# A recurrence's decay from tanh and exp instead of a reciprocal, and sigmoids as tanh of half the argument

## The chip, the cores and the metric

The kernel runs on one NeuronCore of a Trainium2 chip. Each core has a matrix engine (TensorE, PE in the profile; PEld is its weight load), a vector engine (VectorE, DVE), an engine for functions by table (ScalarE, ACT), GpSimd (POOL), and SyncE (SP), whose queue issues most of the transfers here. Each engine works through its own list of instructions in order, and waits on semaphores for the others. The metric is the device time of one execution in microseconds (us), as the median of several runs.

## The reference

One layer of a streaming encoder on 512 frames of 1024 channels, all in float32: a gated token mixer, then a retrieval over 16384 small experts, each added to the residual, and a last RMS norm. The change lies in the second half of the mixer's heads, a gated linear recurrence over the frames:

```python
def rg_lru(xr, w_r, b_r, w_i, b_i, lam):
    b, s, _ = xr.shape
    xh = xr.reshape(b, s, N_LRU_HEADS, LRU_HD)
    r = jax.nn.sigmoid(jnp.einsum('bshi,hij->bshj', xh, w_r) + b_r).astype(jnp.float32)
    i = jax.nn.sigmoid(jnp.einsum('bshi,hij->bshj', xh, w_i) + b_i).astype(jnp.float32)
    log_a = -LRU_C * r * jax.nn.softplus(-lam.astype(jnp.float32))
    a = jnp.exp(log_a)
    u = jnp.sqrt(-jnp.expm1(2.0 * log_a)) * (i * xh.astype(jnp.float32))
...
    _, h = lax.associative_scan(combine, (a, u), axis=1)
    return h.reshape(b, s, LRU_W).astype(xr.dtype)
```

So h(t) = a(t) h(t-1) + u(t), with the decay a between 0 and 1 and u scaled by the root of 1 - a squared. The retrieval that follows scores 128 keys on two sides for each of 8 heads, takes the best 16 pairs, and sums the chosen experts.

## The kernel before

The program has four parts on the time line: a prologue (the frames' norm, the first part of the conditioning vector), the mixer, the scores and searches with the first expert products, and the products with the second expert table.

The mixer keeps channels on the 128 partitions and the 512 frames in the free dimension. Its input projection has 20 blocks of 128 output channels. A block is 24 matmuls of 128x512: weights and input are split into a high and a low part, and the loop over 8 slices of input channels makes three products each (`mm3`, lines 89 to 91: high by high, high by low, low by high). The loop of line 359 goes over four channel blocks `cb` of 128; each takes five of the 20 weight blocks, `px` (the recurrence's input), `pgr` (its output gate), `pc`, `pxa` and `pb` (the short convolution's three). They land in PSUM tiles `ps_z`, of which there are three. A weight block is loaded by SP (line 70, `wraw`), its high part copied by ACT (line 75, `whi`), its low part made by DVE (line 80, `wlo`); there are four buffers of each.

Inside one `cb` the recurrence runs so: ACT copies `px` (364, 366), DVE adds the four taps of the convolution (368, three operations), ACT and DVE split the sum `xc` (373, 375), TensorE makes the two gate products in `ps_g` (377 to 379), ACT makes the two sigmoids `r` and `ig` (381, 383) and `s` = tanh(sp r) (385), where `sp` is half of 8 softplus(-lambda). From s the decay is a = 2/(1+s) - 1, and the root of 1 - a squared is 2 sqrt(s)/(1+s): DVE takes the reciprocal `q` of 1+s (387, 388), `a` from it (390), and the products for u (392 to 394); ACT takes the square root (391). DVE scans over the frames (396), multiplies with the gelu of `pgr` (397 to 407, tanh form), and `head_norm` (333) squares the result on ACT, averages it over each head by two matmuls (341, 342) and scales it. The results of all heads, split into `ybuf_h` and `ybuf_l`, are the input of the output projection (428 to 435).

Beside this stands the rest of the conditioning vector. Its last third (`ada_group(2)`) is summed on DVE: a block `wacc` loaded (line 135) and scaled (151), then seven blocks `wada` added to it (153, three buffers), then a product with ones on TensorE (139), a copy on ACT (159) and transposes (162); and that twice.

The order of the mixer's instructions on each engine isn't written out: a scheduler of the framework places the instructions by its own estimate of their cost, and each engine then keeps that list. From line 1083 on the order is written by hand. ACT's functions come from tables; where the next one is not in the table set that is loaded, the list holds an ACT_TABLE_LOAD.

Of the kernel before, what the change touches and what calls it, by code (L numbers as in the profile page):

```python
# [8 lines left out]
F32 = mybir.dt.float32  # L9
# [4 lines left out]
AF = mybir.ActivationFunctionType  # L14
OP = mybir.AluOpType
# [19 lines left out]
def block_kernel(ctx, tc, xT, small, w_ada1, w_ada, b_ada, w_in, w_r, w_i, w_out, w_q, keys, uT, u, v, final_g, out):  # L35
    nc = tc.nc
    PS = bass.MemoryType.PSUM

    const = ctx.enter_context(tc.tile_pool(name="const", bufs=1))
# [4 lines left out]
    def sm(name, lo=0, n=None):  # L44
        o, w = SMALL[name]
        return small_sb[:, o + lo:o + lo + (w if n is None else n)]
# [9 lines left out]
    boot.close()  # L56
    iota = const.tile([128, 128], F32, name="iota")
    nc.gpsimd.iota(iota, pattern=[[1, 128]], base=0, channel_multiplier=0, allow_small_or_imprecise_dtypes=True)
    const.tile([128, 24], F32, name="pad")
    ones = const.tile([128, 1], F32, name="ones")  # L60
    nc.vector.memset(ones, 1.0)
    sel2 = const.tile([128, XB], F32, name="sel2")
# [195 lines left out]
    sp = const.tile([128, 4], F32, name="sp")  # L258
# [21 lines left out]
    nc.vector.tensor_scalar(z_, lam, -1.0, 0.0, op0=OP.mult, op1=OP.max)  # L280
    nc.vector.tensor_scalar(ac, ac, 8.0, None, op0=OP.mult)
    nc.vector.scalar_tensor_tensor(sp, z_, 4.0, ac, op0=OP.mult, op1=OP.add)
    g2d = dram.tile([2, 512], F32, name="g2d")
    mx = ExitStack()
    mixp = mx.enter_context(tc.tile_pool(name="mixp", bufs=1))
# [33 lines left out]
    def zblock(n, name):  # L319
        i = order.index(n)  # L320
        for j in range(i, min(i + ZL + 2, len(order))):
            if order[j] not in raws:
                raws[order[j]] = load_w(w_in[order[j]])
        for j in range(i, min(i + ZL, len(order))):
            if order[j] not in zsp:
                zsp[order[j]] = split_w(raws[order[j]])
        hi, lo = zsp[n]
        ps = psZ.tile([128, T], F32, name=name, bufs=3)
        mm3(ps, hi, lo, hx, lx, range(KB), True, True)
        next(ada_it, None)  # L330
        return ps
# [27 lines left out]
    for cb in range(4):  # L359
        px = zblock(12 + cb, "ps_z")  # L360
        if pend:
            head_norm(*pend.pop())
        mt = lambda n: mix.tile([128, T], F32, name=n)
        nc.scalar.activation(xpad[:, 3:], px, AF.Copy)
        xc = mt("xc")
        nc.scalar.activation(xc, px, AF.Identity, scale=sm("cbw", cb * 4 + 3, 1), bias=sm("cbb", cb, 1))
        for k in range(3):
            nc.vector.scalar_tensor_tensor(xc, xpad[:, k:k + T], sm("cbw", cb * 4 + k, 1), xc, op0=OP.mult, op1=OP.add)
        pgr = zblock(16 + cb, "ps_z")
        pg = psZ.tile([128, T], F32, name="ps_g", bufs=2)  # L370
        pi = psZ.tile([128, T], F32, name="ps_g", bufs=2)
        xch = mix.tile([128, T], FR, name="cg")
        nc.scalar.activation(xch, xc, AF.Copy)
        xcl = mix.tile([128, T], FR, name="acc")
        nc.vector.tensor_sub(xcl, xc, xch.bitcast(F32))
        for ps, b in ((pg, cb), (pi, 4 + cb)):
            nc.tensor.matmul(ps, bdh[:, b, :], xch, start=True, stop=False)
            nc.tensor.matmul(ps, bdh[:, b, :], xcl, start=False, stop=False)
            nc.tensor.matmul(ps, bdl[:, b, :], xch, start=False, stop=True)
        r = mt("r")  # L380
        nc.scalar.activation(r, pg, AF.Sigmoid, bias=sm("br", cb, 1))
        ig = mt("ig")
        nc.scalar.activation(ig, pi, AF.Sigmoid, bias=sm("bi", cb, 1))
        s = mt("s")
        nc.scalar.activation(s, r, AF.Tanh, scale=sp[:, cb:cb + 1])
        q = mt("q")
        nc.vector.tensor_scalar(q, s, 1.0, None, op0=OP.add)
        nc.vector.reciprocal(q, q)
        a = mt("r")
        nc.vector.tensor_scalar(a, q, 2.0, -1.0, op0=OP.mult, op1=OP.add)  # L390
        nc.scalar.activation(s, s, AF.Sqrt)
        nc.vector.tensor_mul(xc, xc, ig)
        nc.vector.tensor_mul(xc, xc, s)
        nc.vector.scalar_tensor_tensor(xc, xc, 2.0, q, op0=OP.mult, op1=OP.mult)
        h = mt("ig")
        nc.vector.tensor_tensor_scan(h, a, xc, 0.0, op0=OP.mult, op1=OP.add)
        x2 = mt("x2")
        nc.scalar.activation(x2, pgr, AF.Square)
        gr = mt("gr")
        nc.scalar.activation(gr, pgr, AF.Copy)  # L400
        nc.vector.tensor_scalar(x2, x2, 0.044715, 1.0, op0=OP.mult, op1=OP.add)
        nc.vector.tensor_mul(x2, x2, gr)
        nc.scalar.activation(x2, x2, AF.Tanh, scale=0.7978845608028654)
        nc.vector.scalar_tensor_tensor(x2, x2, 1.0, gr, op0=OP.add, op1=OP.mult)
        y = mix.tile([128, T], F32, name="y", bufs=2)
        pend.append((y, 4 + cb, sm("gnb", cb, 1)))
        nc.vector.scalar_tensor_tensor(y, x2, 0.5, h, op0=OP.mult, op1=OP.mult)
        pc = zblock(4 + cb, "ps_z")
        cg = mix.tile([128, T], F32, name="cg")
        nc.scalar.activation(cg, pc, AF.Copy)  # L410
        pxa = zblock(8 + cb, "ps_z")
        head_norm(*pend.pop())
        nc.vector.tensor_mul(vpad[:, 2:], pxa, cg)
        acc = mix.tile([128, T], F32, name="acc")
        nc.scalar.activation(acc, vpad[:, 2:], AF.Copy, scale=sm("caw", cb * 3 + 2, 1))
        for k in range(2):
            nc.vector.scalar_tensor_tensor(acc, vpad[:, k:k + T], sm("caw", cb * 3 + k, 1), acc, op0=OP.mult, op1=OP.add)
        pb = zblock(cb, "ps_z")
        y = mix.tile([128, T], F32, name="y", bufs=2)
        nc.vector.tensor_mul(y, acc, pb)  # L420
        pend.append((y, cb, sm("gna", cb, 1)))
# [64 lines left out]
    for k in range(KB):  # L486
# [4 lines left out]
                             bias=adac[:, 24 + k:25 + k])  # L491
# [678 lines left out]
    for k in range(CE, len(jobs)):  # L1170
# [6 lines left out]
        else:  # L1177
            q, e = divmod(n, 2)
# [137 lines left out]
```

## Time and profile before

| | us |
|---|---|
| median of 3 runs | 1362.52 (1361.08 to 1362.64) |
| the profiled execution's own time | 1361.49 |
| its span, first to last instruction | 1359.7 |
| busy in the span: PE, DVE, ACT, POOL | 1309.5, 1224.1, 729.4, 510.7 |
| DMA, mean over the span | 324 GB/s |

Times in the trace's rows are us from the span's start. A row of the timeline has start, length, engine, line, operation, output and inputs, shape, count, and in brackets how long the engine sat idle before it, and for whom. Instructions of one engine overlap a little, so that two rows may start closer together than the first is long. The mixer's blocks lie between about 44 and 218 us.

### The profile page before, as it was taken

To read this page: it belongs to the slowest core of one execution; us is meant where nothing else is said; L and a number is where in the kernel's file an instruction comes from. 1 tells how busy PE (TensorE), PEld (TensorE's weight loads), DVE (VectorE), ACT (ScalarE), POOL (GpSimd) and SP (SyncE) were. 2 spreads that over 40 slices of the span, in tenths; PEclk is the share of its full clock that TensorE was granted. 3 is DMA by queue.
4 is the path that set the end of the run, shared out by engine and by line. 5 is a ranking of instruction groups with operands and counts; after the bars stand their busy time and mean duration, and the time that the engine had idled before them with its cause. 6 is when DMAs were issued, how large, how long until landed. Compare 5 with 4: busy or idle time off the path is not lost.

```text
span 1359.7 us, 21251 instructions
## 1 busy us (share of the span) xinstructions
PE 1309.5 (96%) x7432; PEld 1120.9 (82%) x7432; DVE 1224.1 (90%) x2261; ACT 729.4 (54%) x1314; POOL 510.7 (38%) x336
## 2 busy tenths in 40 slices
PE   5999999999999999999999989999999999999996
PEld 2667687777999999999899988788888888888884
DVE  6889975889999999999889659799889889999998
ACT  4666644523576988798669544333333434333433
POOL 0000000000244133436557416577647665554550
PEclk9999998999999999999999999999999999999998
DMA  9676442251789999999999999999999999999993
GB/s 357 233 273 214 126 123 101 69 187 34 244 301 330 334 326 405 395 370 375 417 402 417 416 344 390 392 377 416 413 415 413 415 413 415 411 413 410 393 344 136
DMA packets 149375, 440.57 MB, mean 324 GB/s; under 512 B 14994, under 2 KB 42642, under 8 KB 149268
## 3 DMA queue, kind: packets, MB, share of 16 engines
q1 hardware_dynamic: 102116, 267.75, 52.8%
q0 software_dynamic: 46864, 170.41, 32.2%
q8 instruction: 58, 0.95, 0.3%
q10 hardware_dynamic: 288, 1.05, 0.2%
q14 instruction: 49, 0.40, 0.1%
HBM read 394.07 MB, written 45.09 MB: 323 GB/s over the span
## 4 chain that ended last, share of the span: by engine, by line
PE 59%; DVE 19%; DMA 9%; issue 9%; POOL 2%; ACT 1%; SPq 0%; DVEq 0%; POOLq 0%; ACTq 0%
PE acc L1153 33%; PE ps_z L89 4%; PE ps_z L90 4%; PE ps_z L91 4%; DVE wlo L80 4%; DMA wraw<-in_uT_dram 3%; PE ps_act L89 3%; PE ps_act L91 3%; PE ps_act L90 3%; DMA rows<-in_u_dram,idx_s 3%; DVE scr L880 2%; POOL rows L859 2%; DVE oh L692 2%; DMA wraw<-in_v_dram 1%; PE ps_gt L725 1%
## 5 line engine op out<-in xcount | busy, mean ns | idle before, releaser
L75 ACT ACTIVATE whi<-wraw 128x1024 fp32r<-128x1024 f32 x255 | 269.9, 1059 | 339.2 <-PE acc L1153 154.1
L80 DVE TENSOR_TENSOR wlo<-wraw,whi 128x1024 fp32r<-128x1024 f32 x255 | 310.7, 1219 | 61.2 <-ACT whi L75 60.5
L89 PE MATMUL ps_act<-h,whi 128*128 128x320 f32 x928 | 292.5, 315 | 0.0
L90 PE MATMUL ps_act<-h,whi 128*128 128x320 f32 x928 | 287.6, 310 | 0.0
L91 PE MATMUL ps_act<-h,wlo 128*128 128x320 f32 x928 | 287.6, 310 | 0.0
L859 POOL DMA_INDIRECT rows<-in_u_dram,idx_s x128 | 204.2, 1596 | 159.3 <-DVE scr L880 141.8
L859 POOL DMA_INDIRECT rows<-in_v_dram,idx_s x128 | 204.1, 1595 | 154.6 <-DVE ys L897 130.0
L1153 PE MATMUL acc<-whi,ch 128*128 128x512 f32 x750 | 232.9, 392 | 6.3 <-ACT ch L1039 5.2
L1153 PE MATMUL acc<-whi,cl 128*128 128x512 f32 x750 | 232.5, 391 | 0.0
L1153 PE MATMUL acc<-wlo,ch 128*128 128x512 f32 x750 | 232.1, 391 | 0.0
L89 PEld LDWEIGHTS ps_act<-h,whi 128*128 128x128 f32 x928 | 175.0, 189 | 0.7
L90 PEld LDWEIGHTS ps_act<-h,whi 128*128 128x128 f32 x928 | 174.9, 189 | 0.2
L91 PEld LDWEIGHTS ps_act<-h,wlo 128*128 128x128 f32 x928 | 174.7, 188 | 0.0
L859 POOL DMA_INDIRECT rows<-in_u_dram,idx_b x64 | 96.1, 1502 | 208.9 <-DVE scr L880 143.0
L1153 PEld LDWEIGHTS acc<-whi,ch 128*128 128x128 f32 x750 | 141.5, 189 | 36.3 <-ACT ch L1039 5.9
L1153 PEld LDWEIGHTS acc<-wlo,ch 128*128 128x128 f32 x750 | 141.6, 189 | 29.6
L1153 PEld LDWEIGHTS acc<-whi,cl 128*128 128x128 f32 x750 | 141.4, 189 | 29.7 <-DVE cl L1046 0.3
L897 DVE SCALAR_TENSOR_TENSOR ys<-rows,acts,ys 128x1024 f32<-128x1024 f32 x127 | 162.7, 1281 | 1.4
L880 DVE SCALAR_TENSOR_TENSOR scr<-rows,h2n 128x1024 f16<-128x1024 f32 x128 | 156.4, 1222 | 5.2 <-DMA rows<-in_u_dram,idx_s 3.6
L713 ACT ACTIVATE igh<-oh,gl 128x128 f16<-128x128 f16 x320 | 99.6, 431 | 14.5 <-DVE oh L692 14.4
L453 POOL DMA_DIRECT2D x1d<-xn x8 | 4.5, 569 | 257.8 <-ACT xn L452 257.8
L964 ACT ACTIVATE act<-ps_act 128x320 f32<-128x320 f32 x127 | 55.3, 435 | 77.7 <-PE ps_act L91 44.5
(305 smaller groups left out, 1912.3 us busy)
## 6 DMA issues: line engine op xcount, KB each, us to landing
wraw<-in_uT_dram SPq DMA_DIRECT2D x120, 512.0 KB, 7.4
wraw<-in_v_dram SPq DMA_DIRECT2D x103, 512.0 KB, 13.1
wada<-in_w_ada_dram SPq DMA_DIRECT2D x46, 512.0 KB, 5.4
Gd<-stg SPq DMA_DIRECT2D x46, 512.0 KB, 9.0
Ad<-act SPq DMA_DIRECT2D x48, 320.0 KB, 9.2
act<-Ad SPq DMA_DIRECT2D x48, 320.0 KB, 14.2
raw<-in_v_dram SPq DMA_DIRECT2D x25, 512.0 KB, 13.5
h<-Gd SPq DMA_DIRECT2D x12, 1024.0 KB, 17.8
```

The source lines that it names most:

```text
L75: nc.scalar.activation(hi, raw, AF.Copy)
L80: nc.vector.tensor_sub(lo, raw, hi.bitcast(F32))
L89: nc.tensor.matmul(ps, hi[:, k, :], xh(k), start=first and k == ks[0], stop=False)
L90: nc.tensor.matmul(ps, hi[:, k, :], xl(k), start=False, stop=False)
L91: nc.tensor.matmul(ps, lo[:, k, :], xh(k), start=False, stop=last and k == ks[-1])
L692: nc.vector.tensor_tensor(flat.rearrange("p (q n b) -> p q n b", q=8, b=2), io2[:, None, :, :].to_broadcast(shp), sij[:, a0].rearrange("p ...
L713: nc.scalar.activation(ig[:, 1, k // 2, :, k % 2], of[:, k // 2, 0, :, k % 2], AF.Copy, scale=gl[:, t0 + k:t0 + k + 1])
L859: nc.gpsimd.indirect_dma_start(out=r[:, :], out_offset=None, in_=table, in_offset=bass.IndirectOffsetOnAxis(ap=idxs[:, k:k + 1], axis=0))
L880: nc.vector.scalar_tensor_tensor(scr, rows.pop(n), 1.0, hn, op0=OP.mult, op1=OP.mult, accum_out=dst[:, k:k + 1])
L897: nc.vector.scalar_tensor_tensor(ys, rows.pop(k), acts[:, k:k + 1], ys, op0=OP.mult, op1=OP.add)
L964: nc.scalar.activation(act[c // 2][:, c % 2], ps, AF.Gelu)
L1153: nc.tensor.matmul(accs[b][e], st[:, bs], mv[:, e * 512:(e + 1) * 512], start=first, stop=last)
```

## The change

The decay is written with two functions instead of a reciprocal. With x = 8 softplus(-lambda) r, s = tanh(x/2) and q = exp(-x), (1+q) s = 1 - q, so that a = 1 - (1+q) s is q again, but carries s's accuracy near 1; and 1/(1+s) = (1+a)/2. Both sigmoids become tanh of half the argument: r and ig now hold 2 sigmoid - 1, and the missing "+1" and "/2" are moved into scales and biases (columns `sph`, `spn`, `brh`, `bih`, made once on 128x4) and into the operations that follow. The root is taken of s/4. The pad tile shrinks by the 16 columns that the new columns take, so that other tiles keep their places.

```diff
-    const.tile([128, 24], F32, name="pad")
+    const.tile([128, 8], F32, name="pad")
...
+    rg = const.tile([128, 4, 4], F32, name="rg")
+    sph, spn, brh, bih = (rg[:, i, :] for i in range(4))
+    for dst, src, f in ((sph, sp, 0.5), (spn, sp, -1.0), (brh, sm("br"), 0.5), (bih, sm("bi"), 0.5)):
+        nc.vector.tensor_scalar(dst, src, f, None, op0=OP.mult)
...
         r = mt("r")
-        nc.scalar.activation(r, pg, AF.Sigmoid, bias=sm("br", cb, 1))
+        nc.scalar.activation(r, pg, AF.Tanh, scale=0.5, bias=brh[:, cb:cb + 1])
         ig = mt("ig")
-        nc.scalar.activation(ig, pi, AF.Sigmoid, bias=sm("bi", cb, 1))
+        nc.scalar.activation(ig, pi, AF.Tanh, scale=0.5, bias=bih[:, cb:cb + 1])
         s = mt("s")
-        nc.scalar.activation(s, r, AF.Tanh, scale=sp[:, cb:cb + 1])
+        nc.scalar.activation(s, r, AF.Tanh, scale=sph[:, cb:cb + 1], bias=sph[:, cb:cb + 1])
         q = mt("q")
-        nc.vector.tensor_scalar(q, s, 1.0, None, op0=OP.add)
-        nc.vector.reciprocal(q, q)
+        nc.scalar.activation(q, r, AF.Exp, scale=spn[:, cb:cb + 1], bias=spn[:, cb:cb + 1])
         a = mt("r")
-        nc.vector.tensor_scalar(a, q, 2.0, -1.0, op0=OP.mult, op1=OP.add)
-        nc.scalar.activation(s, s, AF.Sqrt)
-        nc.vector.tensor_mul(xc, xc, ig)
+        nc.vector.scalar_tensor_tensor(a, q, 1.0, s, op0=OP.add, op1=OP.mult)
+        nc.vector.tensor_scalar(a, a, -1.0, 1.0, op0=OP.mult, op1=OP.add)
+        nc.scalar.activation(s, s, AF.Sqrt, scale=0.25)
+        nc.vector.scalar_tensor_tensor(xc, ig, 1.0, xc, op0=OP.add, op1=OP.mult)
         nc.vector.tensor_mul(xc, xc, s)
-        nc.vector.scalar_tensor_tensor(xc, xc, 2.0, q, op0=OP.mult, op1=OP.mult)
+        nc.vector.scalar_tensor_tensor(xc, a, 1.0, xc, op0=OP.add, op1=OP.mult)
```

From the first new lines on, a line n of the kernel before is line n + 4 of the changed one; in the recurrence's own lines the new ones are 385, 387, 389 (r, ig, s), 391 (Exp), 393, 394 (decay), 395 (root), 396 to 398 (u) and 400 (scan). The scheduler places the mixer anew, with the new costs; from the output projection's second half on, all lists are the same as before. Three places of the lists follow.

TensorE in the last block, `cb` 3, around its gate products (`ps_g`) and the second `wacc` product. Before, where `ps_z_1379`, `ps_z_1423` and `ps_z_1476` are the weight blocks 17, 18 and 19:

```order
L91 MATMUL ps_z_1303<-h2_83,wlo_1301 128x512
L89 MATMUL ps_z_1379<-h2_83,whi_1375 128x512
L90 MATMUL ps_z_1379<-h2_83,whi_1375 128x512
L89 MATMUL ps_z_1423<-h2_83,whi_1419 128x512
L90 MATMUL ps_z_1423<-h2_83,whi_1419 128x512
L89 MATMUL ps_z_1476<-h2_83,whi_1472 128x512
L90 MATMUL ps_z_1476<-h2_83,whi_1472 128x512
L377 MATMUL ps_g_1334<-cg_1336,bdh_380 128x512
L377 MATMUL ps_g_1335<-cg_1336,bdh_380 128x512
L139 MATMUL ps_row_946<-wacc_1166,ones_79 1x512 x2
L162 MATMUL ps_row_1408<-ident_73,row_1406 128x128 x4
```

In the changed kernel, where `ps_z_1384` and `ps_z_1428` are the weight blocks 17 and 18:

```order
L91 MATMUL ps_z_1384<-h2_83,wlo_1382 128x512
L381 MATMUL ps_g_1339<-cg_1341,bdh_385 128x512
L381 MATMUL ps_g_1340<-cg_1341,bdh_385 128x512
L89 MATMUL ps_z_1384<-h2_83,whi_1380 128x512
L90 MATMUL ps_z_1384<-h2_83,whi_1380 128x512
L91 MATMUL ps_z_1384<-h2_83,wlo_1382 128x512
L139 MATMUL ps_row_951<-wacc_1171,ones_79 1x512 x2
L89 MATMUL ps_z_1428<-h2_83,whi_1424 128x512
L382 MATMUL ps_g_1339<-acc_1343,bdh_385 128x512
```

The first pairs of three weight blocks stood ahead of the gate products; now nearly all of block 17 stands there (its `wlo` is made earlier on DVE), so that between the first `wacc` product and the gate products there are 97 matmuls of 128x512 where there were 82.

DVE at the same place, around the last of the seven additions to `wacc` (153) and the three convolution taps on `xc` (368; 372 in the changed kernel). Before:

```order
L352 TENSOR_TENSOR ybuf_l<-mfull,ybuf_h 128x512
L368 SCALAR_TENSOR_TENSOR xc<-xpad,small_sb,xc 128x512
L153 SCALAR_TENSOR_TENSOR wacc<-wada,cs,wacc 128x1024
L347 SCALAR_TENSOR_TENSOR sq<-ps_rs,sq 128x512
L368 SCALAR_TENSOR_TENSOR xc<-xpad,small_sb,xc 128x512
L348 SCALAR_TENSOR_TENSOR sq<-sq,mfull 128x512
L368 SCALAR_TENSOR_TENSOR xc<-xpad,small_sb,xc 128x512
L350 SCALAR_TENSOR_TENSOR mfull<-y,small_sb,sq 128x512
L153 SCALAR_TENSOR_TENSOR wacc<-wada,cs,wacc 128x1024
```

In the changed kernel:

```order
L343 SCALAR_TENSOR_TENSOR mt_1281<-sq,mt_1279 128x512
L372 SCALAR_TENSOR_TENSOR xc<-xpad,small_sb,xc 128x512
L153 SCALAR_TENSOR_TENSOR wacc<-wada,cs,wacc 128x1024
L372 SCALAR_TENSOR_TENSOR xc<-xpad,small_sb,xc 128x512
L153 SCALAR_TENSOR_TENSOR wacc<-wada,cs,wacc 128x1024
L351 SCALAR_TENSOR_TENSOR sq<-ps_rs,sq 128x512
L372 SCALAR_TENSOR_TENSOR xc<-xpad,small_sb,xc 128x512
L352 SCALAR_TENSOR_TENSOR sq<-sq,mfull 128x512
```

The last addition has moved ahead of the last tap.

ACT in the recurrence of `cb` 3. Before, from the second sigmoid on (`cg` is the copy of the next block's `pc`):

```order
L383 ACTIVATE ig<-ps_g,small_sb 128x512
L385 ACTIVATE s<-r,sp 128x512
L403 ACTIVATE x_1363<-x_1363 128x512
L391 ACT_TABLE_LOAD
L391 ACTIVATE s<-s 128x512
L75 ACTIVATE whi<-wraw 128x1024
L410 ACTIVATE cg<-ps_z 128x512
L75 ACTIVATE whi<-wraw 128x1024
L335 ACTIVATE sq<-y 128x512
```

In the changed kernel:

```order
L387 ACTIVATE ig<-ps_g,rg 128x512
L389 ACTIVATE s<-r,rg 128x512
L391 ACTIVATE q<-r,rg 128x512
L407 ACTIVATE x_1368<-x_1368 128x512
L414 ACTIVATE cg<-ps_z 128x512
L395 ACT_TABLE_LOAD
L395 ACTIVATE s<-s 128x512
L419 ACTIVATE acc<-vpad,small_sb 128x512
L75 ACTIVATE whi<-wraw 128x1024 x2
L339 ACTIVATE sq<-y 128x512
```

The Exp (391) has come in, without a table load of its own, and the copy `cg` now stands ahead of the root and its table load.

## The prediction, made before the changed kernel ran

> **What bounds the kernel now.** I read the busy shares first, then the mixer's stretches, then TensorE's timeline where a stretch is not full. From the page:
>
> ```profile
> span 1359.7 us, 21251 instructions
> PE 1309.5 (96%) x7432; PEld 1120.9 (82%) x7432; DVE 1224.1 (90%) x2261; ACT 729.4 (54%) x1314; POOL 510.7 (38%) x336
> ```
>
> The change touches the recurrence of the mixer, which stands in four channel blocks (cb 0 to 3). The busy times by stretch (columns: stretch, length, then busy us and instructions of PE, PEld, DVE, ACT, POOL; granted clock; DMA share; GB/s):
>
> ```profile
> 100.00:150.00 50.00, 49.64 (x219) 39.04 (x216) 48.42 (x61) 32.54 (x47) 0.00 (x0) 1.00 0.63 208
> 150.00:158.00 8.00, 5.04 (x22) 2.56 (x21) 8.00 (x14) 5.36 (x8) 0.00 (x0) 1.00 0.00 1
> 158.00:218.00 60.00, 60.00 (x270) 49.59 (x268) 41.57 (x52) 27.71 (x37) 0.00 (x0) 1.00 0.41 123
> 220.00:240.00 20.00, 17.66 (x88) 11.89 (x87) 14.01 (x29) 12.82 (x22) 2.70 (x5) 0.83 0.26 93
> ```
>
> The mixer belongs to TensorE. DVE is crowded (48.42 of 50 us), but a shorter DVE list is worth only the time in which TensorE stands still, and that is almost all between 150 and 158 us. There TensorE's timeline reads:
>
> ```profile
> 150.35 0.39 PE L89 MATMUL ps_z<-h,whi 128*128 128x512 f32 x1
> 150.58 0.39 PE L90 MATMUL ps_z<-h,whi 128*128 128x512 f32 x1
> 151.95 0.50 PE L89 MATMUL ps_z<-h,whi 128*128 128x512 f32 x1 [0.99 <-ACT gr L400]
> 152.29 0.40 PE L90 MATMUL ps_z<-h,whi 128*128 128x512 f32 x1
> 153.50 0.73 PE L377 MATMUL ps_g<-cg,bdh 128*128 128x512 f32 x2 [0.81 <-ACT cg L373]
> 154.70 1.03 PE L139 MATMUL ps_row<-wacc,ones 128*1 128x512 f32 x4 [0.46 <-DVE wacc L153]
> 156.42 0.66 PE L162 MATMUL ps_row<-ident,row 128*128 128x128 f32 x4 [0.70 <-ACT row L159]
> 156.83 0.48 PE L378 MATMUL ps_g<-acc,bdh 128*128 128x512 f32 x1
> ```
>
> And some 20 us earlier, at the product of the first half of the gate row:
>
> ```profile
> 131.15 1.03 PE L139 MATMUL ps_row<-wacc,ones 128*1 128x512 f32 x4
> 132.11 0.50 PE L89 MATMUL ps_z<-h,whi 128*128 128x512 f32 x1
> ```
>
> Matmuls in a row start 0.23 us apart (150.35, 150.58). From 150.58 to 156.83 are 6.25 us; the work in them is three such starts (0.69), the L377 pair (0.46), the L139 group (0.96, as from 131.15 to 132.11) and the L162 group (156.42 to 156.83, 0.41), 2.5 us. So **3.7 us** are lost, to four waits that all end on a late DVE or ACT. Everything later (searches, expert products, tail) keeps its order, and starts from the mixer's output: what the mixer gains is passed on whole. That is the ceiling; the 0.36 us missing between 100 and 150 are the only other.
>
> **The change: DVE's list.** One block's recurrence now, cb 1, first on DVE, then on ACT:
>
> ```profile
> 89.48 0.69 DVE L392 TENSOR_TENSOR xc<-xc,ig 128x512 f32<-128x512 f32 x1 [0.92 <-ACT ig L383]
> 90.09 0.43 DVE L387 TENSOR_SCALAR q<-s 128x512 f32<-128x512 f32 x1
> 90.55 3.35 DVE L388 RECIPROCAL q<-q 128x512 f32<-128x512 f32 x1
> 93.82 0.63 DVE L393 TENSOR_TENSOR xc<-xc,s 128x512 f32<-128x512 f32 x1
> 94.36 0.41 DVE L390 TENSOR_SCALAR r<-q 128x512 f32<-128x512 f32 x1
> 94.69 0.69 DVE L394 SCALAR_TENSOR_TENSOR xc<-xc,q 128x512 f32<-128x512 f32 x1
> 95.29 0.69 DVE L404 SCALAR_TENSOR_TENSOR x<-x,gr 128x512 f32<-128x512 f32 x1
> 95.89 1.22 DVE L396 TENSOR_TENSOR_SCAN ig<-r,xc 128x512 f32<-128x512 f32 x1
> ...
> 136.08 0.75 DVE L151 TENSOR_SCALAR wacc<-wacc,cs 128x1024 f32<-128x1024 f32 x1 [0.41 <-DMA wacc<-in_w_ada_dram]
> ...
> 152.70 0.75 DVE L350 SCALAR_TENSOR_TENSOR mfull<-y,small_sb,sq 128x512 f32<-128x512 f32 x1
> 153.37 1.28 DVE L153 SCALAR_TENSOR_TENSOR wacc<-wada,cs,wacc 128x1024 f32<-128x1024 f32 x1
> 154.56 0.68 DVE L352 TENSOR_TENSOR ybuf_l<-mfull,ybuf_h 128x512 fp32r<-128x512 f32 x1
> ```
>
> Start to start, the reciprocal costs 3.27 us, a tensor_scalar 0.33 to 0.46, a two-tensor operation 0.60 (with a column as scalar 0.67, L350), and an L153 1.19. Gone per block: L387 and L388, 3.6 us. New: one scalar_tensor_tensor (0.60) for the decay; its tensor_scalar replaces L390, and two products only change form. Net 3.0 us per block, 12 us in all. The four preparing operations on 128x4 stand in the prologue, and nothing asks for them before the first L385: nothing, and no more than four times the shortest row here, 1.6 us, if DVE were the bound there.
>
> **ACT's list, and the cover that goes.**
>
> ```profile
> 56.34 0.69 ACT L381 ACTIVATE r<-ps_g,small_sb 128x512 f32<-128x512 f32 x1 [0.73 <-PE ps_g L379]
> ...
> 88.18 0.69 ACT L381 ACTIVATE r<-ps_g,small_sb 128x512 f32<-128x512 f32 x1
> 88.76 0.68 ACT L383 ACTIVATE ig<-ps_g,small_sb 128x512 f32<-128x512 f32 x1
> 89.33 0.72 ACT L385 ACTIVATE s<-r,sp 128x512 f32<-128x512 f32 x1
> 89.95 0.63 ACT L403 ACTIVATE x<-x 128x512 f32<-128x512 f32 x1
> 90.60 1.28 ACT L391 ACT_TABLE_LOAD   x1
> 91.89 0.63 ACT L391 ACTIVATE s<-s 128x512 f32<-128x512 f32 x1
> ```
>
> The Exp is one more ACTIVATE: between 0.57 us (L383 to L385) and 0.72 (L385 whole), and I take 0.62, the step from L385 to the next. One table load goes, in cb 0 (24 loads on ACT's list instead of 25), 1.28 us, but there ACT waits 0.73 us for TensorE behind it (56.34), so nothing that the block's end sees. Today the square root is done at 92.52, behind the reciprocal's cover, which lasts to 93.82. After the change it is done 0.62 later, at 93.14, and DVE, with only 0.60 + 0.60 + 0.33 us of other work after the Exp, waits for it at L397. From there come two products and the scan: 93.14 + 0.6 + 0.6 + 1.2 = 95.5, against 97.1 now. So of 3.0 us the block's chain gains 1.6; in cb 0, where the copy cg and a weight split stand ahead of the root, about nothing.
>
> **Where TensorE's wait goes.** In cb 2 those 1.6 us let DVE make one more weight remainder (wlo, L80) before 136.08, where it now waits 0.41 us for the wacc load. In the old order that wlo comes only after the last L153; so TensorE starts three weight blocks by their first pair and stalls. In the new order the whole block stands ahead of the gate products: 97 matmuls lie between the L139 group (it ends at 132.11 today) and the L381 pair, where there were 82. TensorE reaches L381 at 132.1 + 97 x 0.2265 (the starts above, unrounded) = 154.1. Its operand: from 136.08 DVE's list up to the third L372 is one L151 (0.7), seven L153 (1.19 each), seven operations of 0.60 and five of 0.67: 16.6 us, so 152.7, 0.2 more for waits; the copy cg on ACT 0.6: 153.5. In time by 0.6 us; and wacc, two operations earlier (151.6), is needed at 155.2. So the 3.7 us are filled with work that must be done anyway: **-3.7**.
>
> The loads: SP's queue has one more w_out load ahead of the last four wada loads. It asks only for a buffer whose wlo now comes before 136; the first wada load behind it waits anyway for the buffer that the first L153 after 136.08 frees. Nothing.
>
> **A new wait.** In cb 3 the root now stands behind the copy cg (L414), which waits for TensorE's next product. From its end, by the rows above and two of the page,
>
> ```profile
> L75 ACT ACTIVATE whi<-wraw 128x1024 fp32r<-128x1024 f32 x255 | 269.9, 1059 | 339.2 <-PE acc L1153 154.1
> L80 DVE TENSOR_TENSOR wlo<-wraw,whi 128x1024 fp32r<-128x1024 f32 x255 | 310.7, 1219 | 61.2 <-ACT whi L75 60.5
> ```
>
> cg 0.6, load 1.28, root 0.63, then on DVE L397 0.6, acc 0.67, L398 0.6, acc 0.67, scan 1.2, a wlo 1.2, y 0.6, on ACT a square and a copy 1.3, and 0.5 that I guess for hand-overs: 9.8 us. In its new list TensorE has 38 matmuls of 0.2265, 8.6 us, before it asks for the copy (L345). Today cg stands behind the root. The difference is 1.2; bounds 0 and 1.5, and I take **+0.9**, as part of the guess may overlap. The earlier blocks I take at nothing: 0.36 us could be won there, and in cb 2 one more L153 stands ahead of xc, which can cost as much.
>
> The trace has a load and the root's start 1.29 us apart (90.60, 91.89). The Trainium skill ("ScalarE: Activation LUTs", What ACT_TABLE_LOAD costs) states about 2.66 us per switch, a drain of 1.38 us included; by it the new wait would be 1.4 us longer and the time 1361.1; the trace disagrees, with 1.29.
>
> Sum: -3.7 + 0.9 = -2.8. The profiled execution took 1361.49 us (span 1359.7, 1.8 around it), so 1358.7; it lies 1.0 under the median of the runs, 1362.52, and against that median the forecast is **1359.7**.
>
> **The rivals.**
> - *No new wait.* DVE and ACT hand over faster at the end of cb 3: -3.7, 1358.8. For it: 0.5 of the chain's 9.8 us is a guess, and ACT has room. Chance 0.14.
> - *The stall stays.* The root's lost cover puts cb 2's tail past 136.08, so every L153 and xc slides, and L381 waits again. It decides once DVE's list is over 0.6 us late; 2.8 us late gives no change, about 1362.5. For it: the margin is small, and the last four wada loads are each bound to a buffer that an L153 frees. Against: 1.6 us gained ahead of it. Chance 0.25.
> - *A dearer table load.* Cost it twice its row at the new wait, that would be 0.9 + 1.3 = 2.2: 1361.0. The rows 90.60 and 91.89 speak against it. Chance 0.02.
> - *Slower.* The loop of cb 3 (TensorE's product, cg, root, scan, y, L345) becomes the bound: each us that y comes later stops TensorE one us at the in-order L345. From 3.7 us of wait on the kernel loses. If ACT's two weight splits ahead of y's square (2 x 1.06), their wlo on DVE (2 x 1.2) and the next load (1.28) all fall into the loop, its wait is 1.2 + 5.8 = 7.0 and the change +3.3: 1365.8. Against it: most of these stand in the shadow of TensorE's own 8.6. Chance 0.09.
> - *The forecast:* 0.50.
>
> The stretch 220 to 240 has a granted clock of 0.83, just behind the mixer, where TensorE is thin: 20 x 0.17 = 3.4 us of clock lost. No row shows whether the change shifts that; I let the range reach 1 us, some third of it, further on the fast side. The Trainium skill ("TensorE: Matmul & The Clock Gate", Part 1) says that the gate judges by free-running windows of 3.4 us; by that such a drop would come longer or shorter by one window, 1.7 us at half clock, whatever the kernel.
>
> **How the numbers follow.** About 0.2% (2.7 us) is what a measurement of this kernel can tell from no change, and the forecast sits on that edge. Faster: all of the first rival and 0.36 of the forecast's 0.50, since +0.9 may be less: 0.50. Same: the rest of it (0.14), the stall, the load: 0.41. Slower 0.09. The range goes from 1357.5 (4.0 gained with some of the 0.36, and 1 for the clock) to 1363.0 (the stall stays, and half a us of scatter); outside are the slower case and a little.
>
> **What would show it.** Right: TensorE without a wait over 0.3 us between 145 and 160, the L381 pair near 154, DVE waiting for the root at L397 in three or four blocks, some 12 us less DVE time, 24 table loads, a wait of about 1 us at the last block's L345, and the last w_out product some 3 us earlier (near 214). Wrong: a wait at L381 or at the wacc product again; or a mixer that ends 3 us earlier while the time stays, which would refute that its gain is passed on.

## The result, and the profile after

The changed kernel took 1353.02 us (median of 6 runs, 1349.65 to 1360.19), the kernel before 1362.51 on the same chip (6 runs, 1361.08 to 1363.35): a ratio of 0.9950, 95% interval 0.9932 to 0.9967. The forecast was 1359.7, the range 1357.5 to 1363.0: the kernel gained more than the range allows. With six more runs of the changed kernel from the first experiment and 88 of the kernel before from all of them, the means are 1353.8 and 1360.8: 7.0 us faster, 1.8 either way at 95%. (The runs come from several chips; the kernel before has means from 1360.2 to 1361.3 on the four that its later runs used.) That is the figure to be explained.

The profiled execution of the changed kernel is its slowest run, 1360.19 (span 1358.4). Its page:

```profile
span 1358.4 us, 21255 instructions
PE 1307.9 (96%) x7432; PEld 1121.0 (83%) x7432; DVE 1213.9 (89%) x2261; ACT 730.1 (54%) x1317; POOL 507.9 (37%) x336
```

DVE has 10.2 us less, ACT 0.7 more, TensorE 1.6 less. The same stretches as before (columns: stretch, length, then busy us and instructions of PE, PEld, DVE, ACT, POOL; granted clock; DMA share; GB/s):

```profile
100.00:150.00 50.00, 50.00 (x223) 40.01 (x220) 47.19 (x61) 33.08 (x47) 0.00 (x0) 1.00 0.67 211
150.00:158.00 8.00, 8.00 (x37) 5.67 (x37) 7.47 (x13) 4.71 (x8) 0.00 (x0) 1.00 0.00 1
158.00:218.00 60.00, 59.28 (x278) 48.80 (x277) 40.65 (x56) 31.00 (x43) 1.86 (x4) 1.00 0.39 119
220.00:240.00 20.00, 19.69 (x109) 13.59 (x109) 13.67 (x25) 15.17 (x25) 0.54 (x1) 0.91 0.11 42
```

TensorE now fills the 8 us from 150 to 158 (37 matmuls instead of 22), and the clock behind the mixer was granted at 0.91 instead of 0.83. In TensorE's timeline the operations that were waited for, the last product of block 17 (L91), and the two of `head_norm` at the end of cb 3, none with an idle time in brackets:

```profile
130.54 1.03 PE L139 MATMUL ps_row<-wacc,ones 128*1 128x512 f32 x4
...
153.66 0.64 PE L381 MATMUL ps_g<-cg,bdh 128*128 128x512 f32 x2
...
154.59 0.39 PE L91 MATMUL ps_z<-h,wlo 128*128 128x512 f32 x1
154.91 1.03 PE L139 MATMUL ps_row<-wacc,ones 128*1 128x512 f32 x4
...
157.13 0.60 PE L162 MATMUL ps_row<-ident,row 128*128 128x128 f32 x4
...
171.41 0.46 PE L345 MATMUL ps_rs<-mt,sqa 128*128 128x512 f32 x1
...
172.63 0.40 PE L346 MATMUL ps_rs<-mt,sqa 128*128 128x512 f32 x1
```

The last matmul of the output projection in the kernel before, and then in the changed one:

```profile
217.17 0.39 PE L91 MATMUL ps_z<-ybuf_h,wlo 128*128 128x512 f32 x1
```

```profile
212.81 0.39 PE L91 MATMUL ps_z<-ybuf_h,wlo 128*128 128x512 f32 x1
```

So TensorE leaves the mixer 4.36 us earlier. But this run ended only 1.3 us earlier. Where it lost the rest is seen at 650 us, in the waits of TensorE between 600 and 900 us (columns: engine, what waits, for whom; us in all, times, longest), of the changed kernel and then of the kernel before:

```profile
PE ps_gt L729 <- ACT igh L717: 6.0, 1, 6.0
PE acc L1157 <- ACT ch L1043: 5.0, 2, 3.0
```

```profile
PE acc L1153 <- ACT ch L1039: 5.2, 2, 2.7
PE ps_gt L725 <- ACT igh L713: 3.2, 2, 2.8
```

To follow one run against another, I took TensorE's matmuls in the order of their lists and subtracted their start in the first profile of the kernel before (extra matmuls of an experiment left out; "e9 edits" are the calmed later places below). A minus is a lead, in us; the columns are places on that first profile's time line:

```
                        131    150    158    211    235    600    700    900   1300
changed, first        -0.61  -1.00  -4.41  -4.35  -5.74  -5.79  -0.81  -2.14  -1.31
changed, again        -1.19  -1.57  -4.99  -4.93  -7.83  -7.96  -8.44 -10.71 -10.71
changed + delay       +0.39   0.00  -3.41  -3.34  -1.69  -1.76  -2.05  -1.19  -1.19
before + delay        -0.47  -0.59  -0.62  -0.59  +2.54  +2.54  +2.07  +2.71  +2.71
before, again         +0.07  +0.28  +2.52  +2.86  +1.52  +1.42  +1.03  -0.88  -0.11
changed, e9 edits     -1.65  -2.03  -5.44  -5.37  -8.26  -7.65 -12.07  -9.72  -7.47
before, e9 edits      -0.88  -0.77  -0.82  -0.81  -3.70  -3.22  -7.67  -2.59  -1.55
```

From 131 to 158 us each profile of the changed mixer gains 3.8 us. What it has ahead of 131 us (0.61 in the first) isn't firm, for there the profiles of the old mixer differ among themselves by up to 0.9. The lead that TensorE has at 235 us holds to 600 us within 0.6 us. Between 600 and 900 us it changes by several us, in either direction, at three places (near 650, 800 and 866 us; with the e9 edits near 740 as well), and after 1000 us not at all.

### The profile page after: what moved, and what is told of

The parts are those of the page before. It is cut to its first block, busy times and chain, and to the rows that moved or that the text cites. A ratio compares the mean times of both kernels' runs of the same rounds, so it can differ in the third digit from the quotient of the medians.

```text
span 1358.4 us, 21255 instructions
## 1 busy us (share of the span) xinstructions
PE 1307.9 (96%) x7432; PEld 1121.0 (83%) x7432; DVE 1213.9 (89%) x2261; ACT 730.1 (54%) x1317; POOL 507.9 (37%) x336
## 4 chain that ended last, share of the span: by engine, by line
PE 50%; issue 15%; DVE 14%; POOL 10%; DMA 9%; ACT 1%; SPq 0%; DVEq 0%; POOLq 0%; ACTq 0%
PE acc L1157 24%; POOL rows L863 10%; PE ps_z L89 5%; PE ps_z L90 5%; PE ps_z L91 5%; DMA rows<-in_u_dram,idx_s 3%; DVE wlo L80 3%; DMA wraw<-in_v_dram 2%; DMA wraw<-in_uT_dram 2%; PE ps_act L89 2%; PE ps_act L90 2%; PE ps_act L91 2%; DVE scr L884 2%; DVE oh L696 1%; PE ps_row L139 1%
## 5 line engine op out<-in xcount | busy, mean ns | idle before, releaser
L91 PE MATMUL ps_act<-h,wlo 128*128 128x320 f32 x928 | 288.0, 310 | 0.0
L863 POOL DMA_INDIRECT rows<-in_v_dram,idx_s x128 | 198.8, 1553 | 160.7 <-DVE ys L901 137.0
L91 PEld LDWEIGHTS ps_act<-h,wlo 128*128 128x128 f32 x928 | 175.1, 189 | 0.0
L89 PE MATMUL ps_z<-h,whi 128*128 128x512 f32 (+1 forms) x232 | 92.6, 403 | 3.1 <-ACT h L242 2.7
```

What stands on the lines that cost most here:

```text
L89: nc.tensor.matmul(ps, hi[:, k, :], xh(k), start=first and k == ks[0], stop=False)
L91: nc.tensor.matmul(ps, lo[:, k, :], xh(k), start=False, stop=last and k == ks[-1])
L863: nc.gpsimd.indirect_dma_start(out=r[:, :], out_offset=None, in_=table, in_offset=bass.IndirectOffsetOnAxis(ap=idxs[:, k:k + 1], axis=0))
```

## The experiments

All extra matmuls named below write a tile that nobody reads.

**The changed kernel again.** 

> The changed kernel once more, unaltered, for a second profile and more times. In its first profile TensorE ended the mixer 4.35 us earlier than before and ran 5.7 us ahead at 250 us, but only 1.3 us ahead at the end. Theory A (the mixer's gain is handed on whole, what is lost or won behind it is scatter): median 1355.5 to 1358, no single run more than 6 us under the median of before except by chance. Theory B (the stretch from 600 to 900 us, in which the DMA queues are full, adds a gain of its own because it starts earlier): median 1351 to 1355 as in the first six runs, and a profile that shows TensorE further ahead at 900 us than at 250 us.

Measured: 1354.20 (1350.79 to 1354.95), ratio 0.9952 (0.9938 to 0.9966). The profiled run, the fastest of the six, leads by 7.8 us at 235 us and by 10.7 at the end. Both theories have something: the lead grew behind 600 us in this run as B says, but shrank in the first profile. The median lies in B's range. Against my expectation the difference between the two profiles of one kernel starts at 211 to 235 us, where both did the same work.

**A delay behind the mixer**, in the changed kernel and in the kernel before.

```diff
-        hi, lo = split_w(oraw[m])
+        hi, lo = split_w(oraw[m]); psd = [psZ.tile([128, T], F32, name="ps_g", bufs=2)] if m == KB - 1 else []; [nc.tensor.matmul(p, bdh[:, 0, :], ybuf_h[:, 0, :], start=(i == 0), stop=(i == 19)) for p in psd for i in range(20)]
```

> The changed kernel with 20 extra matmuls of 128x512 ahead of the last w_out block (their result is not used), at 0.227 us from one to the next: 4.5 us that put the stages behind the mixer back to where they started before the change. Theory A (gain made in the mixer, handed on whole): 4.5 us slower than the changed kernel alone, about 1357.5. Theory B (most of the gain comes from an earlier start of the stretch from 600 to 900 us): all of the gain goes, 1361 to 1364. Theory C (that stretch waits for its transfers anyway and takes up a delay): within 1.5 us of the changed kernel alone.

> The kernel before with the same 20 extra matmuls at the same place, 4.5 us. Theory A: 1367.0, the whole delay comes out at the end. Theory B (the later stretch answers to the moment at which it starts): another sum than 4.5, by 2 us or more in either direction. Theory C (a delay is taken up by waits for transfers): 1362.5 to 1364.

The extra group in the first of them:

```profile
208.62 4.70 PE L435 MATMUL ps_g<-ybuf_h,bdh 128*128 128x512 f32 x20
```

Measured: 1360.53 (0.9994 of before, 0.9983 to 1.0006) and 1364.24 (1.0030, 1.0019 to 1.0041). By the medians the same 4.5 us cost 6.3 us in the changed kernel and 3.0 in the kernel before. The first refutes C and lies near B's 1361, the second lies between A's 4.5 and C's 1.5; their mean, 4.65, is A's. Inconclusive, and the reason to look for something that makes single results scatter by 2 us. The two kernels differ in the mixer alone, so they also measure the change: the means of 12 runs each are 1360.2 and 1364.7, 4.5 us apart, 1.1 either way at 95%, and the mixer's own lead is 4.4.

**Half speed.** It lies in the clock. TensorE's idle time behind the mixer was 2.33 to 2.35 us in every profile that has not filled it, with the same three waits, but the half-speed stretch that followed was 6.8 us long, 3.4, or none. In each profile all half-speed stretches begin on one grid of 3.41 us, and that grid lies differently in every run. On the grid of its run, the windows behind the mixer are, in the first profile of the kernel before:

```profile
221.05:224.45 3.40, 1.52 (x12) 1.09 (x10) 2.05 (x7) 1.26 (x2) 1.11 (x3) 1.00 0.90 305
224.45:227.87 3.42, 3.22 (x14) 1.72 (x15) 3.42 (x7) 1.95 (x4) 0.00 (x0) 0.50 0.41 162
227.87:231.28 3.41, 3.41 (x10) 2.74 (x10) 1.75 (x4) 2.83 (x5) 0.54 (x1) 0.50 0.19 77
```

and in the second profile of the changed one:

```profile
215.78:219.20 3.42, 1.82 (x12) 1.39 (x12) 1.81 (x6) 1.15 (x3) 1.45 (x3) 1.00 0.83 262
219.20:222.60 3.40, 2.88 (x19) 2.00 (x20) 3.40 (x8) 2.87 (x6) 0.00 (x0) 1.00 0.52 204
```

The first number behind the length is TensorE's busy time, the third from the end the clock: 1.52 of 3.40 us busy is followed by half speed, 1.82 of 3.42 is not. From this I formed theory L, and asked it of both halves of the change, of the kernel before, and of a filled gap.

**Half of the change.** In the first kernel the reciprocal stays and only the gates are Tanh; in the second the gates are Sigmoid and only the decay is new. The main lines of each, against the changed kernel:

```diff
         s = mt("s")
         nc.scalar.activation(s, r, AF.Tanh, scale=sph[:, cb:cb + 1], bias=sph[:, cb:cb + 1])
         q = mt("q")
-        nc.scalar.activation(q, r, AF.Exp, scale=spn[:, cb:cb + 1], bias=spn[:, cb:cb + 1])
+        nc.vector.tensor_scalar(q, s, 1.0, None, op0=OP.add)
+        nc.vector.reciprocal(q, q)
...
```

```diff
-        nc.scalar.activation(r, pg, AF.Tanh, scale=0.5, bias=brh[:, cb:cb + 1])
+        nc.scalar.activation(r, pg, AF.Sigmoid, bias=sm("br", cb, 1))
...
-        nc.scalar.activation(q, r, AF.Exp, scale=spn[:, cb:cb + 1], bias=spn[:, cb:cb + 1])
+        nc.scalar.activation(q, r, AF.Exp, scale=spn2[:, cb:cb + 1])
...
```

> Half of the change: the two gates as Tanh of half the argument, the decay still by the reciprocal. If the gain is VectorE's relief from the reciprocal and the order that follows from it: none of it, 1360 to 1363, with TensorE waiting 3 to 4 us between 150 and 158 us as before. If it is the Tanh form with its one table load less: 1353 to 1356 and no such wait.

> The other half: the decay from Tanh and Exp without the reciprocal, the gates still by Sigmoid, so that ScalarE changes its table more often (four loads more than the changed kernel has). If VectorE's relief makes the gain and ScalarE has room: 1353 to 1357, TensorE without a wait between 150 and 158 us. If the table loads at 1.29 us each come onto the path of the gates: 1358 to 1363, with waits of TensorE for ScalarE in the mixer.

Measured: 1362.08 (1.0008, 0.9996 to 1.0020) and 1355.05 (0.9947, 0.9931 to 0.9963). The Exp half makes the gain; its dearer ScalarE list (29 table loads against the changed kernel's 24) costs at most about a us. The stretch 150 to 158, of the Tanh half and of the Exp half:

```profile
150.00:158.00 8.00, 5.05 (x15) 1.95 (x15) 6.30 (x11) 4.43 (x8) 0.00 (x0) 0.73 0.00 1
```

```profile
150.00:158.00 8.00, 8.00 (x36) 5.65 (x35) 8.00 (x11) 5.51 (x9) 0.00 (x0) 1.00 0.00 1
```

The wait is there in the first and gone in the second; and in the first the clock has fallen as well.

**Without the reciprocal.** In the kernel before, the line with the reciprocal is left out, nothing else.

> The kernel before with the reciprocal of the decay left out (the values of the recurrence are then others), and nothing else: VectorE has 3.3 us less work in each of the four column blocks, ScalarE's work and the table loads stay. If the gain is VectorE's relief and the order of the work that the scheduler makes of it: 5 to 10 us faster, 1352 to 1357, with no wait of TensorE over 0.5 us between 150 and 160 us. If it hangs on the Tanh form of the gates or on the table load that went: within 2 us of 1362.5.

Measured: 1357.43 (0.9964, 0.9948 to 0.9981), TensorE full from 150 to 158 us, and the mixer's last matmul at 213.61. The time is just above the 1352 to 1357 expected. VectorE's relief alone is enough to move the list.

**The kernel before again.** 

> The kernel before, unaltered, for a second profile. In six profiles so far each half-speed stretch of TensorE began where a window of 3.41 us on one grid had held 0.53 or less of busy TensorE, and the grid lies differently in every run. Theory L (lottery): the same 2.3 us of idle time behind the mixer costs 0, 1 or 2 half-speed windows; and the waits of before between 150 and 158 us, the busiest window of which was seen at 0.52 and 0.69, cost one in 6 of 10 positions of the grid, which the changed kernel never pays. Expected: idle behind the mixer 2.3 us again, half-speed windows on one grid again, each after a window of 0.53 or less; a half-speed window near 155 us with chance 0.6, and then TensorE 1.5 to 3 us later at the mixer's end than in the first profile. Theory A (the clock plays no part there): TensorE at the mixer's end within 0.5 us of the first profile.

Its one run took 1361.38. On its grid, the windows of the mixer's waits and the two behind them:

```profile
150.95:154.36 3.41, 1.60 (x6) 0.60 (x4) 3.41 (x6) 2.46 (x5) 0.00 (x0) 1.00 0.00 0
154.36:157.78 3.42, 2.26 (x6) 0.33 (x6) 3.42 (x6) 0.90 (x3) 0.00 (x0) 0.51 0.00 0
157.78:161.19 3.41, 3.41 (x11) 2.83 (x11) 1.79 (x4) 2.49 (x4) 0.00 (x0) 0.50 0.48 153
```

The same four waits (1.0, 0.8, 0.7 and 0.5 us), and now 6.8 us at half speed behind them: in the table of leads this run loses 2.6 us between 150 and 211 us, which the first profile of the same kernel did not lose. The Tanh half lost 2.9 there. Its emptiest window and the one behind it, and then the emptiest of the first profile of the kernel before:

```profile
150.20:153.60 3.40, 1.52 (x6) 0.59 (x4) 3.22 (x5) 2.37 (x5) 0.00 (x0) 1.00 0.00 0
153.60:157.05 3.45, 2.38 (x7) 0.38 (x7) 2.15 (x4) 0.93 (x2) 0.00 (x0) 0.50 0.00 0
```

```profile
152.76:156.18 3.42, 1.76 (x6) 0.39 (x6) 3.42 (x7) 1.67 (x3) 0.00 (x0) 1.00 0.00 0
```

In the five profiles with these waits whole (the Tanh half's add up to the same 3 us), two windows at half speed came in two, none in three. Two things did not come as expected. Two other half-speed stretches of this run, at 229.55 and 659.63 us, began after windows that held 0.60 and 0.63 by the clock's stamps, not 0.53 or less. And the 2.9 us that the run was behind at 211 us were gone at the end: it took as long as the first profile.

**The gap behind the mixer filled**, in the changed kernel.

```diff
-    rows_of(psr2, rstd2)
+    rows_of(psr2, rstd2); rows_of(psZ.tile([128, T], F32, name="ps_g", bufs=2), rstd2)
```

> The changed kernel with the four row products behind the mixer done twice (the second time into a spare tile that nobody reads), so that 1.1 us of the 1.63 us in which TensorE waits for the first modulated block is filled. No window can then fall to 0.53 of busy time there. Theory L: no half-speed stretch between 215 and 235 us in any run; in 2 of 3 positions of the grid that saves 1.4 to 2.9 us, so the median falls by 1 to 2 us against the changed kernel, to 1352 to 1353.5, and TensorE is 2.5 to 3 us ahead of the first profile of before from 213 us to 235 us beside the mixer's 4.4. Theory A: no change, 1353.5 to 1354.5.

Measured: 1353.64 (0.9940, 0.9924 to 0.9956), no half-speed stretch from 215 to 235 us in its profile, and a lead that grows by 2.9 us there, as it did in the second profile of the changed kernel with the gap open. The emptiest window there and the next:

```profile
216.80:220.20 3.40, 2.20 (x19) 1.89 (x17) 2.08 (x6) 1.49 (x3) 0.88 (x2) 1.00 0.98 323
220.20:223.60 3.40, 3.40 (x21) 2.39 (x22) 3.40 (x7) 2.86 (x5) 0.25 (x1) 1.00 0.31 123
```

No window was emptied to 0.53, as expected, but the gain did not show: the time lies in A's range, and against the 1353.0 and 1354.2 of the changed kernel nothing can be told. In the 11 profiles that leave the gap open it cost no window in six, one in four, two in one, at 1.4 us each some 0.8 us in the mean, which is less than I took and than five runs resolve.

**The later places calmed**, in both kernels: the filled gap, and in the two loops over weight chunks ScalarE's copy of a chunk put behind the gate work.

```diff
-        w_high(k + 3)
         gates_low(8)
+        w_high(k + 3)
...
         w_ahead(k)
-        w_high(k + 3)
         w_low(k + 2)
...
+            w_high(k + 3)
             u_chunk(k, psP)
...
                 v_rest(q + 1)
+            w_high(k + 3)
```

> The changed kernel with the three later places taken out at which TensorE's waits scatter from run to run: the filling products behind the mixer as before this, and in the two loops over the weight chunks the copy of a chunk that is still on its way (L75) is put behind the gate work (igh) and behind the coefficients (ch), so that ScalarE no longer holds those up for a late transfer. If the waits near 650, 800 and 866 us come from that order: waits of TensorE there fall from 8 to 12 us in all to 4 or less, with fewer half-speed windows, 1343 to 1350, scatter smaller. If the transfers themselves set the pace there: the waits come back under another name (TensorE for the weights), 1351 to 1356.

> The kernel before with the same edits behind the mixer, so that against the run of the changed kernel with these edits only the mixer differs. Theory A (the mixer hands on the waits it no longer has, and nothing else): 4.4 us slower than that run. Theory L (the waits of before also cost, in about 6 runs of 10, two half-speed windows in the mixer, 2.5 to 3 us more): 5.5 to 7 us slower, and its own times in two groups some 3 us apart. Theory B (the later stretch answers to its starting moment): more than 7.5 or less than 3.5 us slower.

Measured: 1355.47 (0.9966, 0.9954 to 0.9979) and 1361.96 (1.0014, 1.0002 to 1.0026). The first expectation failed as a better version: the wait at 650 us went (the lead grows from 7.7 to 12.1 us by 700), and came back under another name and later, for DVE:

```profile
PE ps_gt L729 <- DVE igh L710: 4.6, 3, 3.3
PE acc L1157 <- DVE cl L1050: 2.9, 2, 2.7
```

Both kernels are 1 to 2 us slower by these edits. The pair differs only in the mixer, and the means of 12 runs each are 1355.3 and 1361.8, 6.5 us apart, 1.1 either way at 95%: within L's 5.5 to 7, above A's 4.4, and neither under 3.5 nor over 7.5 as B would have it. But it doesn't decide against A. The delayed pair, which also differs only in the mixer, gave 4.5, which is A's figure. The two groups of times that L expected in the second kernel are not seen either; its runs fill 4.4 us, most of them near 1362, and scatter no more than the changed kernel's. And the two profiles, neither with a half-speed stretch in the mixer, are 4.6 us apart at 211 us and 5.9 at the end; the rest came about behind 700 us.

**The old work in another list**: the kernel before, with two extra matmuls in its third block.

```diff
-        nc.vector.tensor_sub(xcl, xc, xch.bitcast(F32))
+        nc.vector.tensor_sub(xcl, xc, xch.bitcast(F32)); cb == 2 and [nc.tensor.matmul(p, ident, xc, start=i == 0, stop=i == 1) for p in [psA.tile([128, T], F32, name="ps_col")] for i in range(2)]
```

> The kernel before, with the reciprocal and all else kept, and two matmuls of 128x512 added in the third column block, whose result nobody reads (some 1 us of extra TensorE work). Because of them the scheduler writes another list for all engines: in the last block the gate products (L377) stand at row 485 instead of 475, behind more of the z products, and the adaptive row's products (L139, L162) at 499 and 519 instead of 476 and 477, nearly where the changed kernel has them (490, 494, 500). If the gain is the place of these products in the list: the waits of 3.7 us between 150 and 158 us are gone, TensorE ends the mixer 2.5 to 4 us earlier than before, 1354 to 1358, with 12 us of reciprocals still on VectorE. If it is VectorE's relief: the waits stay or move, 1360.5 to 1363.

Measured: 1356.54 (0.9968, 0.9951 to 0.9985). Its page and its stretch from 150 to 158:

```profile
PE 1306.7 (96%) x7436; PEld 1118.8 (82%) x7436; DVE 1224.4 (90%) x2261; ACT 729.4 (54%) x1314; POOL 503.7 (37%) x336
```

```profile
150.00:158.00 8.00, 8.00 (x36) 6.44 (x35) 7.92 (x12) 4.86 (x8) 0.00 (x0) 1.00 0.07 27
```

DVE is as loaded as in the kernel before, with all four reciprocals, and the waits are gone all the same; about half of the gain is had without the change. (The two extra matmuls stand in the trace as four rows.) It isn't all, since the extra matmuls take time and this list has waits of 1.0 and 0.3 us at 112 us: the mixer's last matmul starts at 215.77, 1.4 us earlier than before and not the 2.5 to 4 expected.

**The old list with part of the wait filled**: the same line with `cb == 3` and one matmul.

> The kernel before with one matmul of 128x512 (its result unread) put ahead of the last block's gate products, inside the waits between 150 and 158 us; the lists are otherwise the same. It takes some 0.5 us of idle time away, so that the emptiest window of 3.41 us there holds 0.58 of busy time instead of 0.43. Theory L (a window under about 0.54 costs half speed in the next one): no half-speed stretch between 150 and 162 us in any run, so 1 to 1.8 us faster in the mean, 1359 to 1360 against 1360.9, with TensorE's waits in the mixer nearly as long as before. Theory A: no change or up to 0.5 us slower.

Measured: 1359.33 (0.9997, 0.9980 to 1.0014); 1359.4 in the mean. Its profile has no half-speed stretch in the mixer, and waits of 2.1 us are left:

```profile
150.00:158.00 8.00, 5.89 (x24) 2.91 (x23) 8.00 (x13) 5.36 (x9) 0.00 (x0) 1.00 0.03 4
```

The size is L's, but the interval also holds no change: inconclusive by itself.

**The time and the clock apart.** Each run of the experiments has its mean granted clock on record, not only the profiled ones; of the first runs only the changed kernel's have it, hence 6.9 and not 7.0 below. What the clock falls short of 1, times the span, is the time lost to it, at most: a half-speed window counts 1.7 us this way and cost about 1.4. (A single run's clock stands to 0.001, which is 1.4 us.) In the differences of the means, with about 95% either way (us):

| | runs | time | lost to the clock | rest |
|---|---|---|---|---|
| the change | 12 and 88 | 6.9 ± 1.8 | 2.2 ± 1.5 | 4.7 ± 0.9 |
| the change, both kernels with the calmed later places | 12 and 12 | 6.5 ± 1.1 | 1.7 ± 1.4 | 4.8 ± 1.1 |
| the change, both kernels with the delay | 12 and 12 | 4.5 ± 1.1 | 0.0 ± 2.1 | 4.5 ± 1.7 |
| the delay, in the changed kernel | 12 and 6 | 6.5 ± 1.7 | 1.6 ± 2.6 | 4.9 ± 1.9 |
| the delay, in the kernel before | 12 and 27 | 3.9 ± 1.2 | -1.1 ± 1.6 | 5.0 ± 1.2 |

The rest is nearly the same wherever the same thing is compared: 4.5 to 4.8 us for the change, with which TensorE leaves the mixer 4.4 us earlier, and 4.9 and 5.0 for the delay of 4.5. What makes the comparisons differ is the clock. The kernel with the filled wait fits this too: it loses 2.0 us less to the clock (± 1.7) than the runs of the kernel before beside it. Where the lost time lies, at the mixer's waits or at the later ones, the runs without a profile don't tell.

## Why the prediction was wrong

It had the sign and the mechanism and was too small: 2.8 us forecast, 7.0 measured. TensorE left the mixer 4.4 us earlier, and about 2 us more came through the clock.

**The ceiling: the step that failed.** "What the mixer gains is passed on whole. That is the ceiling" is right in its first sentence, as far as the means show: the lead at 235 us is the lead at 600, and with the clock's loss taken out 4.5 to 4.8 us are left at the end. The second sentence failed, and with it the range. I priced the waits at their own length, 3.7 us, since the profile of before grants the clock at 1.00 between 150 and 158. That execution was lucky: its emptiest window held 0.52. In two of five profiles the waits emptied one window of the grid to 0.47 or less, and TensorE lost another 2.6 to 2.9 us at half speed: 1.1 us in the mean by this count. Sliding the grid over the first profile's trace (half speed after a window under 0.54) gives such a window in 2 of 3 positions, an estimate of 1.8 us; with 0.50 or 0.57 for the limit it is 0.45 or 0.78 of the positions. With the 4.4 us by which the mixer itself ends earlier this makes 5.5 to 6.2 us, against 7.0 ± 1.8 in all and 6.5 ± 1.1 and 4.5 ± 1.1 for the two pairs. So a wait can cost more than its length, and the clock's share of the gain is there, 2.2 ± 1.5 us. How much of that share the mixer's waits make in the mean is not shown.

**The clock, taken at the wrong place.** I let the range reach 1 us for the clock behind the mixer. There it is a draw that both kernels make alike, of no, one or two windows; it helped the changed kernel's profiles (0.91 and 1.00 against 0.83), but by the count of 11 profiles it is worth under a us in the mean. The draw that only the kernel before makes stood in the rows that I had: 5.04 busy us in 8.

**The new wait in cb 3: mis-sized, 0 instead of +0.9.** The prediction let the copy cg wait for TensorE's next product, 8.6 us ahead of L345, which would be 162.8. But cg copies block 17, whose last product had started at 154.59. On ACT the copy follows at 161.93 without idle time, 0.9 us before that, and the root comes behind it as forecast:

```profile
160.70 0.81 ACT L391 ACTIVATE q<-r,rg 128x512 f32<-128x512 f32 x1
161.41 0.62 ACT L407 ACTIVATE x<-x 128x512 f32<-128x512 f32 x1
161.93 0.59 ACT L414 ACTIVATE cg<-ps_z 128x512 f32<-128x512 f32 x1
162.54 1.28 ACT L395 ACT_TABLE_LOAD   x1
163.83 0.63 ACT L395 ACTIVATE s<-s 128x512 f32<-128x512 f32 x1
```

From cg's start to TensorE's L345 at 171.41 are 9.5 us; I had 9.8 for the chain. TensorE had work for all of it. This is the rival "no new wait", to which I gave 0.14; without the term the forecast is 1358.8, still inside the range.

**Right: the list.** L381 was reached at 153.66 (forecast 154.1) without a wait, and so were the wacc products and L162. Of the 3.7 us, 3.4 came between 150 and 158, and the 0.4 between 131 and 150 is the only other that the prediction saw there. The Exp took 0.71 us from start to start (160.70 to 161.41), not 0.62; DVE waited for it twice, 1.4 us in all, and for the root at L397 three times, 1.8 us, and TensorE for neither. DVE fell by 10.2 us, not 12.

**The rivals.** The stall did not stay, the root's loop did not become the bound, and a table load costs what its row said: from the load (162.54) to the root (163.83) are 1.29 us.

## What to carry to other kernels

A wait of TensorE can be worth more than its length where it can empty a window of the clock's grid: slide a window of 3.41 us over the trace, and where it can hold 1.6 us of idle time, as these profiles have it, add the half-speed time, weighted by the share of positions, even if the profile at hand shows full speed there. Before explaining what differs between two results, take the time lost to the granted clock out of both. And where a scheduler writes the lists, ask what list an edit makes before pricing its operations: two unused matmuls made about half of this gain with the reciprocal still in place.

## What the runs showed of the hardware

In 14 profiles TensorE fell to half speed 40 times ahead of the tail. With the windows taken 0.25 us earlier than the clock's stamps (an offset chosen because it parts the two best), every window with less than half of its time busy was followed by half speed, and none with more than 0.57; between these both occur. With the stamps themselves both occur from 0.44 to 0.63. A stretch ended after one window that was full or nearly so (0.95), or after two or three where those ahead of the last again held idle time. The Trainium skill ("TensorE: Matmul & The Clock Gate", Part 1) says that the window is free-running, 3413 ns long; the traces agree, 3.41 us in every profile, at another offset in each. It also says that the clock falls after at least one idle window; here half a window was enough (1.52 of 3.40 us busy), and the measurement decides.

The waits near 650, 800 and 866 us are the other source of scatter. In the changed kernel's first profile ACT stood 7 us in front of a weight chunk that was still on its way, with the gate work behind it:

```profile
653.54 1.06 ACT L75 ACTIVATE whi<-wraw 128x1024 fp32r<-128x1024 f32 x1 [7.07 <-DMA wraw<-in_uT_dram]
```

```profile
654.98 2.32 PE L729 MATMUL ps_gt<-igh,oh 128*128 128x128 f16 x15 [6.00 <-ACT igh L717]
```

Why the chunk came that late in one run and not in the others stays open; with the order changed the time came back at other waits.
